# Low parts of mixer weights made by an accumulating transfer, a piece's low products last, and another plan for the order of work

## The chip, the core and the metric

The kernel runs on one core of a Trainium2 chip. The metric is the device time of one execution in microseconds (us), of which the median of several runs is taken. TensorE does the products, VectorE (DVE in the rows) and ScalarE (ACT) work on what lies in SBUF and PSUM, GpSimd (POOL) does small element-wise work and issues a few transfers, SyncE (SP) issues nearly all the others.

## The reference, cut to what matters

A trunk of two layers over 256 tokens of width 1024, all in float32. Of each layer the first statement, the mixer, is what this change is about.

```python
for i in range(DEPTH):                       # 2
    hn = rmsnorm(h, ln_mix[i])
    (g_q, g_k, g_v, g_z, g_a, g_b,
     n_q, n_kc, n_vc, n_ks, n_vs, n_kw, n_vw, n_gate,
     s_q, s_k, s_v) = jnp.split(hn @ w_in[i], SPLIT_POINTS, axis=-1)
    o_gdn = gated_deltanet(g_q, g_k, g_v, g_z, g_a, g_b, ...)   # 6 heads
    o_nsa = native_sparse_attention(n_q, ..., n_gate, ...)      # 6 query heads
    o_sb = stick_breaking_attention(s_q, s_k, s_v)              # 4 heads
    mix = jnp.concatenate([o_gdn, head_rmsnorm(o_nsa, ...), head_rmsnorm(o_sb, ...)], axis=-1)
    h = h + mix @ w_out[i]
    h = h + conv_ffn(rmsnorm(h, ln_ffn[i]), w_up[i], ffn_conv[i], w_down[i])
    gate = jax.nn.sigmoid(rmsnorm(h, ln_ple[i]) @ w_ple_gate[i])
    h = h + gate * rmsnorm(p[i] @ w_ple[i], ple_norm[i])
return rmsnorm(h, ln_final)
```

In `gated_deltanet` the tokens are cut into chunks of 64, and for each chunk and head a unit lower triangular system is solved before the chunks are run through one after the other.

## The kernel before, in words

**Products in three parts.** Float32 accuracy comes from three products of a cheaper type. Weights and activations are split into a high part (`wh_...`, `XH`) and a low part (`wl_...`, `XL`), and each product is high times high, high times low and low times high, added up in PSUM. A weight is read in pieces of 128 x 1024 (512 KB), in a fixed order: `g1` four times, `k` three times, `kcvc`, `g2`, `g3`, then `v v v q q q sq sq sk sk sv sv out ... ple ple` and the pieces of the feed-forward part.

**From memory to TensorE.** `prefetch` issues a piece's load on SyncE into one of five raw buffers (`wr_...`). `split_step` makes its two parts, in halves of 512 columns: ScalarE copies the raw piece into `wh_...`, which rounds it, and VectorE subtracts that from the raw piece into `wl_...`. There are four pairs of buffers for the parts. `take` hands a piece to the products, and sees to it that the next one (`LEAD` = 1) is split as well; `split_some` splits more as long as the clocks of ScalarE and VectorE in the program's own model are not more than `slack` ahead of TensorE's. `split_step` already has a second way to make a low part, for names in `ADDED`, and that tuple is empty: nothing goes that way in the kernel before.

**The order of the work.** Every engine works through its instructions in the order in which they are issued. The order is found when the program is built. Parts of the work are generators: the main one (priority 5) runs the projections, the out projection, the feed-forward part and the gate; others do the delta net (`gdn`, with `inverse` and `tokens` inside it), the sparse attention (`nsa`, `compress`, `cmp`, `heads`, `finish`) and the stick breaking (`sb`, `pair`). Each says what it waits for with `need`, and `drive` takes the ready one of the lowest priority number, by a model of the engines' clocks (`Model`). A projection says `need` once for each of its steps, so that its products fill the time in which the others wait. The numbers for each of the two layers stand in `PLAN`: priorities, `slack`, `fslack` (the slack of the feed-forward part), `early`, and `pace`, by which the projections go first when TensorE has had less to do.

**The substitution.** In `gdn`, `blocks` solves the diagonal 16 x 16 blocks of the triangular systems. It multiplies the products into `A`, writes `A` to memory (`D`), reads it back in another order (`Mb`), does 14 dependent pairs of small VectorE instructions (`prod`, `Tb`), and sends the result through memory once more (`Tq` to `G` to `F`), after which `stages` goes on. These transfers are issued on SyncE by `move`, in the same queue as the weights' loads.

**The order of the three products.** `pieceA` (weights stationary: `k`, `v`, `q`, `sq`, `sk`, and `ga` and `up` of the feed-forward part) and `piecesB` (activations stationary: `g2`, `g3`, `sv`) do the three products of one block of 128 rows after the other, and say `need` of the low part before each block.

Of the kernel before, what the change touches and what calls it, by code (L numbers as in the profile page):

```python
# [18 lines left out]
T = 256  # L19
D = 1024  # L20
KT = D // 128
HD = 64
# [116 lines left out]
def _prep(inp):  # L139

    f = lambda n: np.asarray(inp[n])
    out = {}
    out["x"] = f("x").reshape(T, D)
    out["pT"] = np.ascontiguousarray(
# [10 lines left out]
    for l in range(DEPTH):  # L155
# [10 lines left out]
                 "sq": col["sq"], "sk": col["sk"], "sv": col["sv"],  # L166
                 "out": np.concatenate([{0: wo[:384], 1: wo[768:], 2: wo[384:768].reshape(6, 64, D)[rg].reshape(384, D)}[i]
                                        for i in GROUPS[l]], axis=0),
# [26 lines left out]
class Model:  # L195
# [74 lines left out]
    def add(self, dst, src):  # L270

        t = max(self.clock["pool"], self.region(src)[0].max(), self.region(dst)[0].max()) + 0.8
        self.clock["pool"] = t
        self.landed(dst, src, t + self.ADD)

    ADD = 4.5

    def landed(self, dst, src, t):
        if "DRAM" not in str(src.space):
# [143 lines left out]
class Trunk:  # L423

    PLAN = (dict(pace=1.0, early=0.2, slack=5, fslack=6, step=1, gdn=0, nsa=0, sb=0, inverse=2,
                 tokens=3, out=0, compress=-1, cmp=2, heads=1, finish=1, pair=4),
            dict(pace=1.1, early=0.3, slack=3, fslack=8, step=1, gdn=1, nsa=0, sb=2, inverse=2,
                 tokens=3, out=2, compress=0, cmp=4, heads=3, finish=0, pair=2))  # L430
    WR = 5
    WARM = (14, 0, 1, 1, 1, 0)

    def __init__(self, ctx, tc, I, out, tap=None, depth=DEPTH):
# [32 lines left out]
        self.taken = []  # L467
        self.plan = self.M.plan = self.PLAN[0]
        self.slack = 0
# [178 lines left out]
    def spare(self, n, i):  # L648
        return (n, i) in self.SPARE

    ADDED = ()

    def added(self):
        return self.splitting[4] if self.splitting else self.n_split < len(self.split_seq) and self.by_transfer()

    def by_transfer(self):
        l, n, i = self.split_seq[self.n_split][:3]
        return n in self.ADDED and not self.spare(n, i) and self.n_split >= self.n_take + 2

    def split_to(self, n):  # L660
        while self.n_split < n:
# [6 lines left out]
               and self.split_step()):  # L668
            pass

    LEAD = 1

    def take(self, name, i):
        l = self.n_take // self.per_layer
        p = (l, name, i)
        while p not in self.parts:
            if not self.split_step():
                self.prefetch(now=True)
                assert self.split_step(), p
        self.n_take += 1  # L680
        self.taken.append(p)
        while self.n_split < min(self.n_take + self.LEAD, len(self.split_seq)) and not self.hold and self.split_step():
            pass
        return self.parts.pop(p)

# [7 lines left out]
    def setup(self):  # L693
        v, cp, I = self.v, self.cp, self.I
        self.table("silu_and_others")
        self.h = self.xp.tile([128, 2, D], F32, name="h")
        for s in self.HS:
# [69 lines left out]
    def row(self, i):  # L767

        while self.n_row <= min(i, 4 * self.depth):
            t = self.cp.tile([128, D], F32, tag="row", name=f"row{self.n_row}")  # L770
            j = self.n_row if self.n_row < 4 * self.depth else 4 * DEPTH
# [164 lines left out]
    def pieceA(self, name, i, out, X, fresh=False):  # L936

        W = self.take(name, i)
        if fresh:
            mm = self.t.matmul  # L940
            for k in range(KT):
                yield self.need(0, W[1], X[0])
                mm(out, W[0][:, k], X[0][:, k], start=k == 0, stop=False)
                mm(out, W[1][:, k], X[0][:, k], start=False, stop=False)
            for k in range(KT):
                mm(out, W[0][:, k], X[1][:, k], start=False, stop=k == KT - 1)
            self.done()
            return
        for k in range(0, KT, self.plan["step"]):
            yield self.need(0, W[1], X[1])  # L950
            self.projA(out, X, W, range(k, k + self.plan["step"]))
        self.done()

    def piecesB(self, name, n, outs, cols, X, nk):
        for i in range(n):
            W = self.take(name, i)
            for t in range(2):
                for k in range(nk):
                    yield self.need(0, W[1], self.of(t))
                    self.projB(outs[t][:, :cols], X, W, t, i * nk, [k])  # L960
            self.done()


# [226 lines left out]
    def gdn(self, l):  # L1190
        v, a, g, gp, c, m = self.v, self.a, self.g, self.gp, self.c, self.m
        mm = self.t.matmul
# [57 lines left out]
        for r, lhs, msk, dst in ((r1, "incl", "m_strict", dec), (r2, "gt", "m_incl", decT)):  # L1250
            for x in range(2):
# [3 lines left out]
                   start=False, stop=True)  # L1255
# [15 lines left out]
        def chunks(b, src, x):  # L1271

            for u, cp in units:
                t, hp = divmod(u, 3)
                o = t * 128 + cp * 64
                mm(b[P[cp], u * 64:u * 64 + 64], kn[P[x], hp, o:o + 64], src[P[x], hp, o:o + 64], start=True, stop=True)
# [3 lines left out]
        def blocks():  # L1280


            n = 24 * (64 // NB)
            M = gp.tile([n, NB, NB], F32, tag="h45_0", name="Mb")
            Tb = gp.tile([n, NB, NB], F32, tag="h45_1", name="Tb")
            g.memset(Tb, 0.0)
            g.memset(Tb.rearrange("p i c -> p (i c)")[:, ::NB + 1], 1.0)
            bs = yield self.small(2, kn, dec[0], dec[1])
            for x in range(2):
                chunks(bs[x], kn, x)  # L1290
            D = self.dram.tile([2, 6, 128, 64], F32, name=f"D{l}")
            for x in range(2):
                v.tensor_mul(fl(A[x]), bs[x][:, 0:384], fl(dec[x]))
            self.free(*bs)
            A16 = [H16("A16", "h1", x) for x in range(2)]
            for x in range(2):
                self.copy(A16[x], A[x])
            for x in range(2):
                yield self.need(0, A[x])
                self.move(D[x].rearrange("u p s -> p u s"), A[x])  # L1300
            yield self.need(0, D)
            nb = 64 // NB
            for k in range(nb):
                src = D.rearrange("x u (c b i) (e s) -> (x u c) b e i s", c=2, b=nb, e=nb)[:, k, k]
                self.move(M[k * 24:k * 24 + 24], src)
            prod = gp.tile([n, NB * NB // 4], F32, tag="h6_1", name="prod")
            yield self.need(0, M, Tb)
            for j in range(NB - 1):
                if j and j % 3 == 0:
                    yield self.pause(1)  # L1310
                r, c2 = NB - 1 - j, j + 1
                rows = M[:, j + 1:, j:j + 1]
                if j:
                    p = prod[:, 0:r * c2].rearrange("p (r c) -> p r c", c=c2)
                    v.tensor_tensor(p, rows.to_broadcast([n, r, c2]), Tb[:, j:j + 1, 0:c2].to_broadcast([n, r, c2]), op=OP.mult)
                else:
                    p = rows
                v.tensor_tensor(Tb[:, j + 1:, 0:c2], Tb[:, j + 1:, 0:c2], p, op=OP.subtract)
            G = self.dram.tile([2, 24, 64 // NB, NB, NB], F16, name=f"G{l}")
            F = gp.tile([128, 24, NB], F16, tag="h6_0", name="F")  # L1320
            Tqs = []
            for q in range(2):
                Tq = gp.tile([n, NB, NB], F16, tag=f"h0_{q}", name="Tq", bufs=2)
                v.tensor_copy(Tq, Tb if q == 0 else Tb.rearrange("p i c -> p c i"))
                Tqs.append(Tq)
            for q in range(2):
                yield self.need(0, Tqs[q])
                self.move(G[q].rearrange("r b i c -> b r (i c)"), Tqs[q].rearrange("p i c -> p (i c)"))
            yield self.need(0, G)
            for q in range(2):  # L1330
                self.move(F[:, q * 12:q * 12 + 12], G[q].rearrange("(z c) b i s -> (c b i) z s", c=2))
            yield self.need(0, F)
            return A16, F

        def stages(x, A16, F):
# [182 lines left out]
        for ch in range(4):  # L1518
            t, cp = divmod(ch, 2)
# [475 lines left out]
    def main(self):  # L1995
# [40 lines left out]
        for l in range(self.depth):  # L2036
            self.plan = self.M.plan = self.PLAN[l]
            self.slack = self.plan["slack"]
# [76 lines left out]
```

## Time and profile before

| | |
|---|---|
| median of 3 runs | 837.64 us (837.60 to 843.46) |
| the profiled execution | 837.27 us, of which the span from the first to the last instruction is 835.5 us |
| TensorE busy | 811.6 us, 97% of the span |
| VectorE busy | 626.3 us, 75% |
| ScalarE busy | 478.8 us, 57% |
| GpSimd busy | 77.4 us, 9% |
| mean granted clock of TensorE | 0.984 of full speed |

Busy time is the time in which an engine had an instruction of its own under way. A busy TensorE may still be at half its clock: the rows of stretches give the granted clock, where 1.00 is 2.4 GHz and 0.50 is 1.2 GHz.

### The profile page before, as it was taken

To read this page: it belongs to the slowest core of one execution; us is meant where nothing else is said; L and a number is where in the kernel's file an instruction comes from. 1 tells how busy PE (TensorE), PEld (TensorE's weight loads), DVE (VectorE), ACT (ScalarE), POOL (GpSimd) and SP (SyncE) were. 2 spreads that over 40 slices of the span, in tenths; PEclk is the share of its full clock that TensorE was granted. 3 is DMA by queue.
4 is the path that set the end of the run, shared out by engine and by line. 5 is a ranking of instruction groups with operands and counts; after the bars stand their busy time and mean duration, and the time that the engine had idled before them with its cause. 6 is when DMAs were issued, how large, how long until landed. Compare 5 with 4: busy or idle time off the path is not lost.

```text
span 835.5 us, 16816 instructions
## 1 busy us (share of the span) xinstructions
PE 811.6 (97%) x6529; PEld 736.3 (88%) x6529; DVE 626.3 (75%) x1337; ACT 478.8 (57%) x1043; POOL 77.4 (9%) x151
## 2 busy tenths in 40 slices
PE   8999899999999999999999979999999999999996
PEld 6989778888999999998998868888899999999986
DVE  5748988677887788876775688967588878788755
ACT  6546474556665566554655465627476556566543
POOL 2012000211100000000301100021110000000012
PEclk9999899999999999999999997999999999999999
DMA  8645230235676677753565414203446556676501
GB/s 310 251 163 150 66 110 28 77 123 154 201 227 186 188 214 220 218 189 96 152 233 186 134 69 111 86 27 102 151 152 227 202 181 202 220 209 219 176 30 51
DMA packets 50591, 131.40 MB, mean 157 GB/s; under 512 B 17104, under 2 KB 18000, under 8 KB 50512
## 3 DMA queue, kind: packets, MB, share of 16 engines
q1 hardware_dynamic: 49056, 125.42, 47.4%
q0 software_dynamic: 1312, 4.72, 1.7%
q8 instruction: 51, 0.84, 0.4%
q14 instruction: 28, 0.23, 0.1%
q10 hardware_dynamic: 144, 0.20, 0.1%
HBM read 128.29 MB, written 2.03 MB: 156 GB/s over the span
## 4 chain that ended last, share of the span: by engine, by line
PE 80%; DVE 10%; ACT 4%; DMA 2%; issue 2%; POOL 1%; SPq 0%; POOLq 0%; DVEq 0%; ACTq 0%
PE b L352 80%; DVE wl_g L352 1%; DMA wr_w1v<-in_w_dram 1%; DVE Tb L352 1%; DVE cv L352 1%; DVE prod L352 1%; DVE oq L352 1%; ACT XH L352 1%; DMA wr_g<-in_w_dram 1%; DVE XL L352 0%; DVE QQ L352 0%; DMA wr_q<-in_w_dram 0%; ACT xh L352 0%; ACT wh_g L352 0%; DVE wl_k L352 0%
## 5 line engine op out<-in xcount | busy, mean ns | idle before, releaser
L352 DVE SCALAR_TENSOR_TENSOR u<-b,pc,u 128x255 f32<-128x255 f32 (+1 forms) x176 | 84.7, 481 | 41.1 <-ACT u L352 37.9
L352 PE MATMUL b<-XL,wh_up 128*128 128x256 f32 x352 | 99.7, 283 | 0.0
L352 PE MATMUL b<-XH,wl_up 128*128 128x256 f32 x352 | 99.6, 283 | 0.0
L352 PE MATMUL b<-XH,wh_up 128*128 128x256 f32 x352 | 99.6, 283 | 0.0
L352 PE MATMUL b<-XH,wl_ga 128*128 128x256 f32 x352 | 99.0, 283 | 0.0
L352 PE MATMUL b<-XH,wh_ga 128*128 128x256 f32 x352 | 99.0, 283 | 0.0
L352 PE MATMUL b<-XL,wh_ga 128*128 128x256 f32 x352 | 97.3, 283 | 0.0
L352 ACT ACTIVATE u<-b,pc 128x256 f32<-128x256 f32 x88 | 41.5, 472 | 74.8 <-PE b L352 74.8
L352 PE MATMUL b<-wl_dn,ah 128*128 128x512 f32 x176 | 69.3, 394 | 0.0
L352 PE MATMUL b<-wh_dn,al 128*128 128x512 f32 x176 | 69.2, 393 | 0.0
L352 PE MATMUL b<-wh_dn,ah 128*128 128x512 f32 x176 | 69.2, 393 | 0.0
L352 PEld LDWEIGHTS b<-XH,wh_ga 128*128 128x128 f32 x352 | 66.9, 190 | 1.7
L352 PEld LDWEIGHTS b<-XL,wh_ga 128*128 128x128 f32 x352 | 66.0, 190 | 1.5
L352 PEld LDWEIGHTS b<-XL,wh_up 128*128 128x128 f32 x352 | 67.1, 191 | 0.0
L352 PEld LDWEIGHTS b<-XH,wh_up 128*128 128x128 f32 x352 | 67.1, 191 | 0.0
L352 PEld LDWEIGHTS b<-XH,wl_up 128*128 128x128 f32 x352 | 67.1, 191 | 0.0
L352 PEld LDWEIGHTS b<-XH,wl_ga 128*128 128x128 f32 x352 | 67.0, 190 | 0.1
L352 DVE TENSOR_TENSOR wl_ga<-wr_ga,wh_ga 128x512 fp32r<-128x512 f32 x88 | 56.9, 688 | 6.1 <-ACT wh_ga L352 2.6
L352 DVE TENSOR_TENSOR wl_up<-wr_up,wh_up 128x512 fp32r<-128x512 f32 x88 | 56.6, 685 | 0.4
L352 DVE TENSOR_TENSOR wl_dn<-wr_dn,wh_dn 128x512 fp32r<-128x512 f32 x88 | 56.5, 684 | 0.4
L352 ACT ACTIVATE ah<-sg 128x256 fp32r<-128x256 f32 x44 | 18.4, 418 | 64.8 <-DVE sg L352 64.8
L352 ACT ACTIVATE wh_up<-wr_up 128x512 fp32r<-128x512 f32 x88 | 50.2, 620 | 0.0
(385 smaller groups left out, 2209.7 us busy)
## 6 DMA issues: line engine op xcount, KB each, us to landing
wr_ga<-in_w_dram SPq DMA_DIRECT2D x44, 512.0 KB, 3.8
wr_up<-in_w_dram SPq DMA_DIRECT2D x44, 512.0 KB, 4.2
wr_dn<-in_w_dram SPq DMA_DIRECT2D x44, 512.0 KB, 3.6
wr_out<-in_w_dram SPq DMA_DIRECT2D x16, 512.0 KB, 3.5
wr_pg<-in_w_dram SPq DMA_DIRECT2D x16, 512.0 KB, 3.3
row<-in_rows_dram POOLq DMA_DIRECT2D x8, 512.0 KB, 4.1
wr_g<-in_w_dram SPq DMA_DIRECT2D x8, 512.0 KB, 5.5
wr_g<-in_w_dram SPq DMA_DIRECT2D x8, 414.0 KB, 3.3
```

Of the source, the lines that this page charges most:

```text
L352: return f(*args, **kw)
```

## The change

- `ADDED` names `v`, `q`, `sq`, `sk` and `sv`. For a piece that goes this way ScalarE writes the high part and then its negative into the low part's buffer, and GpSimd issues one transfer of the whole piece that adds the raw piece to it. VectorE does nothing.
- A piece goes this way only if it is at least two pieces behind the next one to be taken, if the model's clock of the loads and of GpSimd is less than `ROOM` = 0.5 us ahead of ScalarE's, and if `quiet` is off. `quiet` is set from the write of `A` until `Mb` is there, and from the tenth step of the substitution until `F` is there.
- With such a piece next, `take` looks three pieces ahead instead of one.
- `Model.add` puts a transfer into the clock of the loads.
- `pieceA` and `piecesB` do all products with the high part of a weight first and those with its low part last, and say `need` of each part on its own, a block at a time.
- `PLAN` has other numbers for both layers.

```diff
@@ Model.add
         t = max(self.clock["pool"], self.region(src)[0].max(), self.region(dst)[0].max()) + 0.8
         self.clock["pool"] = t
-        self.landed(dst, src, t + self.ADD)
-
-    ADD = 4.5
+        self.loaded = t = max(self.loaded, t + 1.2) + 2.7
+        self.landed(dst, src, t + 0.9)
@@ Trunk
-    PLAN = (dict(pace=1.0, early=0.2, slack=5, fslack=6, step=1, gdn=0, nsa=0, sb=0, inverse=2,
+    PLAN = (dict(pace=1.0, early=0.2, slack=2, fslack=6, step=1, gdn=3, nsa=4, sb=0, inverse=0,
                  tokens=3, out=0, compress=-1, cmp=2, heads=1, finish=1, pair=4),
-            dict(pace=1.1, early=0.3, slack=3, fslack=8, step=1, gdn=1, nsa=0, sb=2, inverse=2,
-                 tokens=3, out=2, compress=0, cmp=4, heads=3, finish=0, pair=2))
+            dict(pace=1.2, early=0.05, slack=2, fslack=8, step=1, gdn=1, nsa=1, sb=-2, inverse=2,
+                 tokens=3, out=2, compress=4, cmp=4, heads=3, finish=0, pair=4))
...
-    ADDED = ()
+    ADDED = ("v", "q", "sq", "sk", "sv")
+
+    ROOM = 0.5
+    quiet = False
...
     def by_transfer(self):
         l, n, i = self.split_seq[self.n_split][:3]
-        return n in self.ADDED and not self.spare(n, i) and self.n_split >= self.n_take + 2
+        return n in self.ADDED and not self.spare(n, i) and not self.quiet and self.n_split >= self.n_take + 2 \
+            and max(self.M.loaded, self.M.clock["pool"]) < self.M.clock["act"] + self.ROOM
...
-    LEAD = 1
+    LEAD = 3
@@ take
-        while self.n_split < min(self.n_take + self.LEAD, len(self.split_seq)) and not self.hold and self.split_step():
+        while self.n_split < min(self.n_take + (self.LEAD if self.added() else 1), len(self.split_seq)) and not self.hold and self.split_step():
             pass
@@ pieceA
-        for k in range(0, KT, self.plan["step"]):
-            yield self.need(0, W[1], X[1])
-            self.projA(out, X, W, range(k, k + self.plan["step"]))
+        mm = self.t.matmul
+        for k in range(KT):
+            yield self.need(0, W[0], X[1])
+            for x in X:
+                mm(out, W[0][:, k], x[:, k], start=k == 0 and x is X[0], stop=False)
+        for k in range(KT):
+            yield self.need(0, W[1])
+            mm(out, W[1][:, k], X[0][:, k], start=False, stop=k == KT - 1)
         self.done()
@@ piecesB
+        mm = self.t.matmul
         for i in range(n):
             W = self.take(name, i)
-            for t in range(2):
-                for k in range(nk):
-                    yield self.need(0, W[1], self.of(t))
-                    self.projB(outs[t][:, :cols], X, W, t, i * nk, [k])
+            for q, xs in ((0, X), (1, X[:1])):
+                for t in range(2):
+                    s = slice(t * 128, t * 128 + 128)
+                    for k in range(nk):
+                        yield self.need(0, W[q], self.of(t))
+                        self.M.part = t
+                        for x in xs:
+                            mm(outs[t][:, :cols], x[:, i * nk + k, s], W[q][:, k], start=(q, i, k) == (0, 0, 0) and x is X[0],
+                               stop=(q, i, k) == (1, n - 1, nk - 1))
+                        self.M.part = None
             self.done()
@@ gdn, blocks
             D = self.dram.tile([2, 6, 128, 64], F32, name=f"D{l}")
+            self.quiet = True
...
             yield self.need(0, M, Tb)
+            self.quiet = False
             for j in range(NB - 1):
+                self.quiet = j >= 9
...
             yield self.need(0, F)
+            self.quiet = False
             return A16, F
```

## Rows read from the trace of the kernel before

**Rows 1.** The page: the span and the busy time of each engine.
```profile
span 835.5 us, 16816 instructions
PE 811.6 (97%) x6529; PEld 736.3 (88%) x6529; DVE 626.3 (75%) x1337; ACT 478.8 (57%) x1043; POOL 77.4 (9%) x151
```
**Rows 2.** Stretches: from:to, length, busy time (instructions) by engine, clock, DMA share, GB/s.
```profile
20.00:81.00 61.00, 60.66 (x450) 55.61 (x449) 39.84 (x100) 34.40 (x74) 7.59 (x14) 1.00 0.60 199
81.00:113.00 32.00, 28.05 (x185) 23.45 (x186) 30.23 (x92) 16.85 (x41) 1.37 (x3) 0.89 0.32 89
113.00:170.00 57.00, 56.21 (x868) 48.80 (x867) 42.19 (x109) 32.29 (x64) 8.02 (x14) 1.00 0.19 58
...
485.00:512.00 27.00, 21.93 (x127) 18.76 (x127) 25.45 (x77) 11.18 (x27) 0.92 (x2) 0.75 0.26 67
...
612.00:800.00 188.00, 188.00 (x1324) 176.63 (x1325) 150.80 (x282) 113.62 (x241) 3.81 (x8) 1.00 0.61 197
```
**Rows 3.** Stretches of the first layer's mixer, the same columns.
```profile
94.00:98.00 4.00, 1.95 (x14) 1.43 (x12) 3.69 (x14) 2.55 (x5) 0.00 (x0) 1.00 0.07 20
98.00:105.00 7.00, 6.27 (x27) 5.33 (x28) 6.76 (x18) 2.78 (x7) 0.91 (x2) 0.51 0.63 129
105.00:108.00 3.00, 2.10 (x13) 1.27 (x12) 2.83 (x8) 0.87 (x3) 0.40 (x1) 1.00 0.73 231
```
**Rows 4.** Stretches of the second layer's mixer, the same columns.
```profile
485.00:494.00 9.00, 8.56 (x69) 7.84 (x68) 8.25 (x25) 3.71 (x7) 0.00 (x0) 1.00 0.01 4
...
494.00:499.00 5.00, 0.39 (x3) 0.19 (x3) 4.55 (x20) 2.35 (x7) 0.00 (x0) 0.84 0.01 2
499.00:511.00 12.00, 11.98 (x50) 9.73 (x51) 11.65 (x33) 5.12 (x15) 0.50 (x2) 0.50 0.58 147
```
**Rows 5.** Waits of TensorE, the whole run: in total, times, longest (us).
```profile
PE b L352 <- DVE mx L352: 4.6, 1, 4.6
PE b L352 <- DVE cq L352: 1.7, 1, 1.7
```
**Rows 6.** VectorE's groups, 81 to 113 us, then 485 to 512: busy us, mean ns.
```profile
L352 DVE TENSOR_TENSOR wl_q<-wr_q,wh_q 128x512 fp32r<-128x512 f32 x4 | 2.6, 682 | 0.0
L352 DVE TENSOR_TENSOR wl_sk<-wr_sk,wh_sk 128x512 fp32r<-128x512 f32 x4 | 2.6, 685 | 0.0
L352 DVE TENSOR_TENSOR wl_sq<-wr_sq,wh_sq 128x512 fp32r<-128x512 f32 x4 | 2.6, 681 | 0.0
...
L352 DVE TENSOR_TENSOR wl_q<-wr_q,wh_q 128x512 fp32r<-128x512 f32 x4 | 2.6, 683 | 0.0
L352 DVE TENSOR_TENSOR wl_sq<-wr_sq,wh_sq 128x512 fp32r<-128x512 f32 x3 | 1.9, 687 | 0.0
```
**Rows 7.** ScalarE's copies: a group of 485 to 512 us; the chain near 480 us.
```profile
L352 ACT ACTIVATE wh_q<-wr_q 128x512 fp32r<-128x512 f32 x4 | 2.3, 620 | 0.0
...
480.49 1.14 ACT wh_q L352 x2
```
**Rows 8.** The substitution by its tiles: duration min/median/max ns, first and last start us.
```profile
L352 DVE TENSOR_TENSOR prod<-Mb,Tb x28: 172/206/222, 85.3 to 496.8; 96x28 f32<-96x28 f32 x4, 96x39 f32<-96x39 f32 x4, 96x48 f32<-96x48 f32 x4, 96x55 f32<-96x55 f32 x4
L497 SPq DMA_DIRECT2D Mb<-D x8: 322/415/430, 66.9 to 472.9; - x8
```
**Rows 9.** GpSimd's loads of 512 KB by their tile: issue in ns, landing in us.
```profile
L772 POOL DMA_DIRECT2D row<-in_rows_dram x8: 613/635/788, 17.3 to 808.0; - x8
DMA to landing us min/median/max: 3.9/4.1/7.4
```
**Rows 10.** TensorE in order of time, 84 to 89 us: start, duration, operation.
```profile
84.68 0.28 PE L352 MATMUL b<-XH,wh_q 128*128 128x256 f32 x1
...
87.80 0.28 PE L352 MATMUL b<-XH,wl_q 128*128 128x256 f32 x1
...
88.27 0.36 PE L352 MATMUL b<-XH,wh_q 128*128 128x256 f32 x1
88.47 0.28 PE L352 MATMUL b<-XL,wh_q 128*128 128x256 f32 x1
```

## The prediction

> **What bounds the kernel now.** I read the page first. TensorE is busy for 811.6 of 835.5 us, and no other engine for more than 75% [rows 1], so time can only be won where TensorE stands or runs at its lower clock. The stretches come next. In the feed-forward part it works without a gap at full clock, 188.00 of 188.00 us in the second layer [rows 2]; one of two such rows stands, for the first layer's is alike. In the mixers two stretches stand out. From 81 to 113 us it is busy for 28.05 of 32 us at a mean clock of 0.89, from 485 to 512 us for 21.93 of 27 us at 0.75, and in both VectorE is nearly full: 30.23 of 32 and 25.45 of 27 us [rows 2]. What follows is full again, 56.21 of 57 us at clock 1.00 [rows 2]; so is the stretch behind the second one (again one of two rows).
>
> A finer cut prices them. First layer: TensorE stands for 2.05 us in 94 to 98, 0.73 in 98 to 105 and 0.90 in 105 to 108, and 6.27 busy us run at 0.51 [rows 3]. That is 2.4 GHz in part and 1.2 in the rest, mostly the latter: 6.27 x 0.49 = 3.1 us lost to the clock, 3.7 to waiting, together 6.8. Second layer: 4.6 us of standing in 494 to 499, then 11.98 busy us at 0.50, so 6.0 lost to the clock, together 10.6 [rows 4]. The clock fell each time after TensorE had stood. The sum, 17.4 us, is all that the change can win in these stretches: 837.27 - 17.4 = 819.9. The waits say for what TensorE stood: 4.6 us for VectorE's `mx`, 1.7 for its `cq` [rows 5]. Both are instructions that came late in a full queue, behind the substitution among others.
>
> **The change, part by part.**
>
> *Subtractions leave VectorE.* In 81 to 113 us it makes 12 half low parts of `q`, `sq` and `sk`, 12 x 0.68 = 8.2 us (7.8 within the stretch), in 485 to 512 us seven, 4.5 us [rows 6]. At best all go. At worst none does: a piece has to be two behind the next one taken, with four pairs of buffers and one piece in use, so only one or two can be eligible at a time, and `quiet` shuts the way from `A` to `Mb` and again from the tenth step to `F`. What is left open during the substitution are its first nine steps, about 9 x 2 x 0.24 = 4 us of VectorE's queue (206 ns each and a gap, [rows 8]).
>
> *What TensorE could do meanwhile.* From 485 to 494 us ScalarE is busy for 3.71 of 9 us, the transfers for 1% [rows 4]. A piece's 24 products of 256 columns are 0.12 us apart (27 of them from 84.68 to 87.80 us, [rows 10]), so 2.9 us. Two pieces of `q` made there would be 5.8 us of work, more than the 4.6 us of standing, and all of the 10.6 us would come back. With one piece, 2.9 us are filled; the rest, 1.7 us, is like the first layer's 2.05, after which still 3.1 us went to the clock [rows 3]: 2.9 + (6.0 - 3.1) = 5.8 us. Ends 0 and 10.6; I take 8, between one and two pieces. In the first layer one piece covers the 2.05 us, but the nine subtractions behind it lie mostly where `quiet` forbids transfers until `F`. Ends 0 and 6.8; I take half, 3.4. Sum: 11.4 us won.
>
> *What is added on ScalarE.* Two more copies a piece, nearest row 0.62 us each [rows 7]. In the full stretches ScalarE has room (16.85 of 32 and 11.18 of 27 us, [rows 2]), which hides them. Without cover they cost 1.24 us a piece: near 480 us the copies of `wh_q`, 1.14 us, stand on the chain ahead of the attention's operands [rows 7]. Ends 0 and 2.4 a layer; I take 0.6, so 1.2.
>
> *The transfers.* Issue on GpSimd takes 0.61 to 0.79 us; a plain load of 512 KB from there lands after 3.9 to 7.4 us, mostly 4.1 [rows 9]. No row shows one that adds. It moves at least as much as a load and reads a second operand, so its ends are 3.9 and twice the slowest, 14.8; sooner than a load is excluded. I take 5, nearest to the median load. There is time for that: two pieces ahead, 5.8 us, and 16 products of the piece itself, 1.9 us, make 7.7; less copies and issue (1.24 and 0.64) 5.8 us are left. So nothing is lost, but only by 0.8 us. GpSimd waits at the transfer for ScalarE's copies, and behind it in the queue wait the additions of the rope, the products of the delta state and the norms' powers, with VectorE waiting for those; GpSimd is busy for 9% [rows 1], and I take nothing, at worst 1.2 us a piece. The raw buffer stays held some 5 us longer. The next load waits for it on SyncE, and the substitution's own transfers are queued behind that load. From 485 to 494 us that queue carries nothing [rows 4].
>
> The Trainium skill (SBUF — State Buffer, Who interferes with whom) speaks against transfers from GpSimd: their descriptors are written through a port that VectorE can hold for a whole instruction in its two-port modes. The eight issues in [rows 9] took 0.61 to 0.79 us, so the trace does not bear out a long wait. By the rule an issue would wait for at most one such instruction, some tenths of a microsecond by estimate, which would bring the 0.8 us down and makes the late transfer below a little likelier.
>
> *Low products last.* The three kinds take equally long and each has its own weight load, so the order alone costs nothing in the full stretches, the feed-forward part among them (1324 products in 188 us, [rows 2]). It lets TensorE begin 1.9 us before a low part is there. Steps become shorter: two products or one instead of three. After another kind of work the first product takes 0.20 us instead of 0.12 [rows 10], so every added return to the projections costs 0.08. Ends: none, or 30 returns, 2.4 us; I take 0.6.
>
> *The plan.* The first layer's substitution comes forward. Its data is asked for at 66.9 us (issue of `Mb`), but its first `prod` starts at 85.3 [rows 8], because the attention's operands were put ahead. With `inverse` at 0 and `nsa` at 4 it can start up to 14 us sooner, while VectorE has room: from 20 to 81 us it is busy for 39.84 of 61, and TensorE for 60.66 [rows 2]. That supports the half which I took. It delays the sparse attention by the substitution's 10 us, which the projections can cover. `slack` 2 instead of 5 and 3 leaves VectorE's queue shorter, and also fewer pieces ready ahead. I can't price an order that I don't see: at best it brings the rest of the 17.4 us, at worst a new stall of the size of the second layer's, 10.6 us. I take nothing.
>
> Sum: 837.27 - 11.4 + 1.2 + 0.6 = 827.7 us. The profiled execution lies 0.37 us below the median of 837.64, so **828 us**.
>
> **The rivals.**
>
> *The relief changes nothing* (time 835, 832 to 841). Pieces are not eligible when it counts, or the stall only moves: with the projections used up earlier, `mx`, the convolutions and the substitution still follow each other on VectorE, and a later stretch starves. For it: in 485 to 498 us VectorE did no subtraction at all, so removing subtractions can't shorten that queue; and the second layer's `inverse` stays at 2. Against it: TensorE stood although ScalarE and the transfers were idle, just what the second way uses. It would give the 3.4 us of one layer or less, 834 to 838.
>
> *The transfer comes late* (time 848). If it lands more than 5.8 us after its issue, TensorE stands at the low products, in order, with everything behind it. At 7.4 us, the slowest row, that is 1.6 us for each piece; with 9.5 pieces in the two stretches (19 half parts, [rows 6]) 15 us. Since 2 us of standing was enough to bring the clock down [rows 3], some 5 us more go to the clock. 828 + 15 + 5 = 848. It decides from 5.8 us of landing on, and is worth more than the gain from about 6.8. For it: two operands and a queue shared with weight loads. Against it: the transfers were 1% busy from 485 to 494 us.
>
> *It does not do what it says*: no transfer at all. Then the order and the plan act alone, within the first rival's span; it is counted there.
>
> **How the numbers follow.** A measurement of this kernel can tell about 1%, 8.4 us, from no change, so faster means below 829.2 and slower above 846. Forecast (820 to 833 us): 0.55, of which 0.40 below 829.2, since its middle lies there and the ends of the second layer are nearer to the full 10.6 than to none. The relief that changes nothing: 0.25, all within 1%. Late transfers: 0.20, above 846. Together faster 0.40, same 0.40, slower 0.20. The range takes in the ceiling (819.9, and 0.9 for the unknown plan) and the second rival; late transfers stay outside: 819 to 846.
>
> **What would show it.** Right: `wl_q`, `wl_sq`, `wl_sk` or `wl_sv` written by GpSimd's transfers, five to ten a layer; fewer VectorE subtractions near the substitution; no waits of several us for `mx` or `cq`; no stretch of 12 us at 0.50 in the second layer; the first `prod` well before 85 us. Wrong: TensorE waiting for a `wl` from a transfer (late); the same number of subtractions (not done); TensorE standing after 150 or after 550 us, where it is full now (the stall moved); ScalarE's copies ending the chain ahead of the attention. A landing time of 8 us or more, or fewer than three transfers a layer, would make the forecast wrong.

## The result and the profile after

The changed kernel takes 834.48 us (median of 20 runs, 831.96 to 839.93), the kernel before 837.85 us beside it (20 runs). The ratio is 0.9941, with a 95% interval of 0.9915 to 0.9966: a gain of 0.6%, within the 1% that was called no change. Executions of one program differ with their mean granted clock: of 35 of the kernel before, measured beside no_transfers, 16 took 836.1 to 838.0 us at 0.983 to 0.987 and 12 took 842.9 to 844.4 us at 0.977 or 0.978. The profiled execution took 832.23 us. The forecast of 828 was too low, and the time is that of the first rival (835).

The page of the kernel after, first its span and engines, which answer to [rows 1]:

```profile
span 830.4 us, 16809 instructions
PE 805.0 (97%) x6529; PEld 730.2 (88%) x6529; DVE 622.2 (75%) x1332; ACT 482.6 (58%) x1048; POOL 80.3 (10%) x156
```

VectorE is busy for 4 us less than its 626, ScalarE for as much more. Then the stretches of the kernel after, with the columns of [rows 2]:

```profile
81.00:113.00 32.00, 28.97 (x310) 24.56 (x311) 30.17 (x91) 18.88 (x46) 2.27 (x5) 1.00 0.25 60
485.00:512.00 27.00, 26.37 (x234) 22.80 (x234) 24.61 (x58) 21.18 (x47) 1.47 (x3) 1.00 0.41 116
575.00:590.00 15.00, 9.24 (x29) 6.09 (x28) 7.41 (x17) 3.67 (x9) 2.72 (x4) 0.67 0.32 107
612.00:800.00 188.00, 187.75 (x1322) 176.08 (x1321) 148.49 (x278) 111.45 (x239) 3.63 (x9) 1.00 0.60 193
```

Both stretches that cost 17.4 us before are nearly mended: the clock is 1.00 in each, TensorE stands for 3.03 us in the first and 0.63 in the second. That is 3.7 us left, 13.7 won; in the first stretch most of what is won is the clock's 3.1 us, since 3.03 us of standing are left of 3.95. The third row is new. From 575 to 590 us TensorE stands for 5.76 us, and 9.24 busy us run at 0.67 (3.0 us lost), together 8.8. In the kernel before this stretch was full:

```profile
575.00:590.00 15.00, 15.00 (x94) 12.78 (x93) 11.16 (x24) 10.24 (x25) 3.11 (x5) 1.00 0.33 108
```

13.7 won and 8.8 given back leave 4.9, and the span is 5.1 us shorter. The feed-forward row is as full as before. TensorE's longest wait of the kernel after is no longer for `mx` [rows 5] but for the last output of the delta net, followed by short ones:

```profile
PE b L351 <- DVE zs L351: 3.3, 1, 3.3
PE b L351 <- ACT XH L351: 1.8, 5, 0.7
PE b L351 <- ACT wh_q L351: 1.6, 1, 1.6
```

**Why 575 to 590 starves.** The substitution of the kernel after answers to [rows 8], and two later tiles of the delta net's chain stand beside it, the state `S` and the gated output `zs`:

```profile
L351 DVE TENSOR_TENSOR prod<-Mb,Tb x28: 171/206/242, 76.2 to 481.8; 96x28 f32<-96x28 f32 x4, 96x39 f32<-96x39 f32 x4, 96x48 f32<-96x48 f32 x4, 96x55 f32<-96x55 f32 x4
L351 DVE TENSOR_TENSOR S<-S,b x4: 347/355/356, 148.1 to 566.1; 128x192 f32<-128x192 f32 x4
L351 DVE TENSOR_TENSOR zs<-oq,zs x8: 357/358/358, 154.2 to 584.6; 128x192 f32<-128x192 f32 x8
```

The same two tiles of the kernel before:

```profile
L352 DVE TENSOR_TENSOR S<-S,b x4: 348/353/354, 159.7 to 557.2; 128x192 f32<-128x192 f32 x4
L352 DVE TENSOR_TENSOR zs<-oq,zs x8: 357/358/358, 168.8 to 583.2; 128x192 f32<-128x192 f32 x8
```

In the first layer everything comes sooner. In the second the last `prod` starts 15.0 us sooner (481.8 for 496.8), but the last `S` starts 8.9 us later and the last `zs` 1.4 later. TensorE used the head start up on projections: the last product with `wl_sv` starts at 555.2 us, where before it started at 577.1. When the projections were done it had to wait for `zs`, as late as ever, which the out projection takes before stick breaking's rows. VectorE's order of time in the kernel after shows where the delta net stuck (a gap in brackets is idle time and what ended it):

```profile
549.67 0.63 DVE L351 TENSOR_TENSOR vn<-uu,b 64x192 f32<-64x192 f32 x2
553.50 0.55 DVE L351 TENSOR_REDUCE hss<-hsq 128x6 f32<-128x384 f32 x1 [3.20 <-ACT hsq L351]
555.80 0.86 DVE L351 TENSOR_TENSOR o<-o,hss 128x384 f32<-128x384 f32 x1 [1.74 <-POOL hss L351]
556.67 1.95 DVE L351 SCALAR_TENSOR_TENSOR L<-b,L 128x384 f32<-128x384 f32 x4
558.54 0.75 DVE L351 TENSOR_TENSOR pl<-pT,ph 128x256 fp32r<-128x256 f32 x2
559.20 2.49 DVE L351 TENSOR_TENSOR wl_out<-wr_out,wh_out 128x512 fp32r<-128x512 f32 x4
561.61 0.35 DVE L351 TENSOR_TENSOR S<-S,b 128x192 f32<-128x192 f32 x1
```

Between `vn` and the `S` that follows it in the chain lie 11.9 us. Two more lines show that VectorE's queue is only half of it. This `S` also needs a product of `vn` on TensorE and a step on GpSimd:

```profile
555.44 0.56 PE L351 MATMUL b<-vn,kk 64*64 64x64 f32 x12
```

```profile
555.74 0.50 POOL L351 TENSOR_TENSOR S<-S,eg 128x192 f32<-128x192 f32 x1
```

The product comes behind 5 us of `sv`'s products in TensorE's order, GpSimd's step behind the sparse attention's norm. So `S` could not go before 556.2 us, and the 4.94 us for which VectorE idles before that norm's two steps are not what held it. From then on it stood for 5.4 us more in VectorE's queue, behind stick breaking (`L`), the low part `pl` and a piece of `out`. Behind the late `zs`, 575 to 590 us gives back 8.8 of the 13.7 us won; TensorE waits for no transfer there.

**What became of the transfers.** The DMA issues of the kernel after, then the issue on GpSimd and ScalarE's negating copies of one tile:

```profile
wl_sk<-wr_sk POOLq DMA_DIRECT2D x2, 512.0 KB, 5.7
wl_sv<-wr_sv POOLq DMA_DIRECT2D x2, 512.0 KB, 4.9
wl_q<-wr_q POOLq DMA_DIRECT2D x1, 512.0 KB, 4.7
```

```profile
L351 ACT ACTIVATE wl_sk<-wh_sk x4: 630/632/633, 110.0 to 119.6; 128x512 fp32r<-128x512 f32 x4
L630 POOL DMA_DIRECT2D wl_sk<-wr_sk x2: 865/898/931, 112.1 to 120.6; - x2
```

Only five of 24 pieces went that way, three in the first layer and two in the second. In the two stretches VectorE still makes 18 half low parts (8 and 10) where it made 19 [rows 6], and it is as full as before: 30.17 of 32 us, and 24.61 of 27. It was not relieved.

### The profile page after: what moved, and what is told of

It reads as the page before. It is cut to its first block, busy times and chain, and to the rows that moved or that the text cites. A ratio compares the mean times of both kernels' runs of the same rounds, so it can differ in the third digit from the quotient of the medians.

```text
span 830.4 us, 16809 instructions
## 1 busy us (share of the span) xinstructions
PE 805.0 (97%) x6529; PEld 730.2 (88%) x6529; DVE 622.2 (75%) x1332; ACT 482.6 (58%) x1048; POOL 80.3 (10%) x156
## 4 chain that ended last, share of the span: by engine, by line
PE 80%; DVE 9%; ACT 6%; POOL 2%; issue 2%; POOLq 0%; DVEq 0%; ACTq 0%
PE b L351 80%; POOL hss L351 1%; ACT XH L351 1%; DVE oq L351 1%; DVE wl_out L351 1%; DVE XL L351 1%; DVE wl_v L351 1%; POOL ss L351 1%; ACT wh_q L351 0%; ACT L472 0%; ACT KH L351 0%; ACT xh L351 0%; DVE wl_k L351 0%; ACT ctmp L351 0%; DVE ck L351 0%
## 5 line engine op out<-in xcount | busy, mean ns | idle before, releaser
L351 PE MATMUL b<-XH,wh_up 128*128 128x256 f32 x352 | 86.4, 283 | 0.0
L351 PE MATMUL b<-XL,wh_up 128*128 128x256 f32 x352 | 86.4, 283 | 0.0
L351 PE MATMUL b<-XH,wh_ga 128*128 128x256 f32 x352 | 86.2, 282 | 0.0
L351 PE MATMUL b<-XL,wh_ga 128*128 128x256 f32 x352 | 84.6, 283 | 0.0
L351 PE MATMUL b<-XH,wl_ga 128*128 128x256 f32 x352 | 51.1, 283 | 0.0
L351 ACT ACTIVATE wh_dn<-wr_dn 128x512 fp32r<-128x512 f32 x88 | 50.2, 621 | 0.0
L351 ACT ACTIVATE wh_ga<-wr_ga 128x512 fp32r<-128x512 f32 x88 | 50.1, 617 | 0.0
L351 PE MATMUL b<-XH,wl_up 128*128 128x256 f32 x352 | 49.4, 283 | 0.0
```

Source lines behind the costliest of these rows:

```text
L351: return f(*args, **kw)
```

## The experiments

All ratios are to the kernel before, with 95% intervals. What a stretch loses is TensorE's standing plus its busy time times what the clock lacks, as above.

### Which part makes the gain

**no_transfers**: the kernel after without transfers.

```diff
-    ADDED = ("v", "q", "sq", "sk", "sv")
+    ADDED = ()
```

> The changed kernel with ADDED empty: plan and low products last stay, the five transfers become VectorE subtractions. If the plan made the gain (theory of the order: the changed trace has only five transfers, ten half subtractions of 0.68 us), within 2 us of the changed kernel, ratio to before 0.992 to 0.997. If the transfers made it (theory of the relief, the forecast's), it falls back to before, ratio 0.999 to 1.003, and the stand of 4.6 us for mx with about 12 us at clock 0.50 is there again.

834.51 us (12 runs), 0.9944 [0.9913, 0.9974]: the same as after. The transfers are worth nothing that can be measured, in either direction. But the loss lies elsewhere: 575 to 590 is nearly full here, and a late stall with its stand for `zs` (3.8 us) is in the first layer:

```profile
170.00:190.00 20.00, 15.33 (x80) 11.49 (x80) 11.51 (x27) 7.18 (x15) 4.61 (x6) 0.85 0.30 98
575.00:590.00 15.00, 14.82 (x110) 12.39 (x104) 11.88 (x28) 8.33 (x19) 4.28 (x6) 1.00 0.39 125
```

**plan_only**: the kernel before with the new `PLAN` and nothing else.

```diff
-    PLAN = (dict(pace=1.0, early=0.2, slack=5, ..., gdn=0, nsa=0, inverse=2, ...), dict(...))
+    PLAN = (dict(pace=1.0, early=0.2, slack=2, ..., gdn=3, nsa=4, inverse=0, ...), dict(...))
```

> The kernel before with the new PLAN alone: products in the old order, no transfers, the model without transfers. Theory of the order: most of the gain, ratio 0.992 to 0.998. Theory of the relief: no gain or a loss, ratio 0.999 to 1.010, because the slack of 2 leaves fewer pieces ready and nothing takes work from VectorE.

834.85 us (12 runs), 0.9942 [0.9913, 0.9972]: by the ratio the plan alone gives as much as the whole change. Its profiled execution, 836.88 us, is only 0.4 us below the 837.27 of the kernel before, so the profiles do not bear out a gain of this size. Nor are the stretches the same:

```profile
81.00:113.00 32.00, 28.46 (x211) 24.08 (x210) 26.30 (x76) 14.85 (x38) 1.38 (x3) 0.79 0.28 73
485.00:512.00 27.00, 23.17 (x195) 21.50 (x194) 24.56 (x74) 16.01 (x35) 0.92 (x2) 1.00 0.37 110
```

The second layer's 10.6 us are down to 3.8, the first layer's 6.8 have become 9.5 (3.5 standing, 28.46 x 0.21 of clock); the waits are for VectorE's `wl_q` (5.5 us, three times), which the order of the products then removes.

**low_last_only**: the kernel before with only the new `pieceA` and `piecesB`.

```diff
-            yield self.need(0, W[1], X[1])
-            self.projA(out, X, W, range(k, k + self.plan["step"]))
+            yield self.need(0, W[0], X[1])
+            ... (high products; then the low ones, each behind need(0, W[1]))
```

> The kernel before with the new pieceA and piecesB alone. Theory of the order: the plan is needed, ratio 0.998 to 1.002. Third theory (low products last is what counts, since TensorE can begin a piece 1.9 us before its low part is there): ratio 0.993 to 0.997, and the stand before mx gets shorter by 2 us or more in the second layer.

847.3 us (12 runs), 1.0087 [1.0054, 1.0121]: slower. In the profiled execution the span is 10.6 us longer (846.1), and 8.5 us are lost where the kernel before loses nothing: from 455 to 480 us TensorE is busy for 24.93 us at 0.66, a fall of the clock without a stand (see the end). The order alone also brings new waits, for VectorE's `cv` (3.7 us), `zs` (2.9) and `oq` (1.9), which the kernel before did not have at this length, while 485 to 512 us loses 4.2 us for 10.6. What the shorter steps cost by themselves, for which 0.6 us was taken, is not separated from the clock.

**old_product_order**: the kernel after with the old `pieceA` and `piecesB` (the diff above, turned round).

> The changed kernel with the pieceA and piecesB of before, so a low part is wanted with the first block of its piece; seven pieces go by transfer (sq, sk, sv and q, sk, sv, sv). If low products last is needed to cover the transfers' 5 to 6 us, TensorE stands for a wl from a transfer and the ratio to before is 0.997 to 1.005. Theory of the order: two pieces ahead are cover enough, ratio 0.990 to 0.996, the same as the plan alone (0.994).

837.4 us (12 runs), 0.9974 [0.9940, 1.0007]. With plan and transfers the low products last may be worth 0.3%, but the intervals overlap (0.9940 to 0.9966 lies in both), and without the transfers, plan and old order had 0.9942, so this is not shown. Seven pieces go by transfer here. It waits for `wl_q` again (4.3 us of VectorE's, 0.9 of a transfer's).

**all_but_plan**: the kernel after with the old `PLAN`.

> The changed kernel with the PLAN of before: four transfers (q and sv in each layer), low products last. Theory of the order: no gain, ratio 0.997 to 1.004. Theory of the relief: most of the gain, 0.992 to 0.997, and the stand of the second layer mostly gone.

835.27 us (12 runs), 0.9965 [0.9932, 0.9997]. That is 1.2% below low_last_only's 1.0087, with four transfers and their longer look ahead as the only difference. In 81 to 113 us TensorE is now busy for 29.88 of 32 us at a clock of 1.00 (2.1 us lost), with low last alone for 28.85 at 0.84 (7.8 lost). But low_last_only's profiled execution had lost 8.5 us to its clock from 455 to 480 us, where this one is at 1.00, so how much of the 1.2% the transfers win stays open. By the ratios the parts do not add up: the order costs 0.9% alone and nothing that shows with the rest. And here too a late stall comes, with the old plan: from 170 to 190 us TensorE is busy for 15.04 of 20 us at 0.76, 8.6 us lost, its longest wait `zs` (2.1 us).

### Which layer's plan, and the late stall

**plan_first_layer** (the kernel after, second layer's numbers of before) and **plan_second_layer** (the other way round).

```diff
@@ plan_first_layer
-            dict(pace=1.2, early=0.05, slack=2, fslack=8, step=1, gdn=1, nsa=1, sb=-2, ..., compress=4, ..., pair=4))
+            dict(pace=1.1, early=0.3, slack=3, fslack=8, step=1, gdn=1, nsa=0, sb=2, ..., compress=0, ..., pair=2))
```

> The changed kernel with the new PLAN for the first layer alone; the second layer has the numbers of before. Theory of the order: the first layer's 4 us stay, and the second layer stands neither as before nor at its end: ratio to before 0.988 to 0.996, its late stand for zs at most 2 us. Theory that any plan of the second layer loses the same (the loss only moves): 0.994 to 1.000, with 8 to 12 us of standing and half clock somewhere in the second mixer.

> The changed kernel with the new PLAN for the second layer alone. Theory of the order: the first layer loses its gain again, 6 to 7 us of standing and half clock in 90 to 110 us or later; the second layer ends about as in the changed kernel, with its late stand for zs: ratio 0.995 to 1.002.

The first layer's plan alone took 830.11 us (4 runs), 0.9892 [0.9834, 0.9950], the second layer's alone 832.69 us (10 runs), 0.9920 [0.9892, 0.9948]: neither half needs the other, and the second's result missed its expectation. With the old numbers in the second layer the last `zs` starts at 575.5 us and the late stall is gone, while 485 to 512 us loses 5.2 us again (23.19 of 27 us busy at 0.94):

```profile
575.00:590.00 15.00, 14.95 (x69) 11.98 (x68) 8.91 (x19) 7.44 (x15) 2.41 (x4) 1.00 0.41 132
```

With the old numbers in the first layer the stall goes to 170 to 190 us instead (15.53 of 20 us busy at 0.74). There 575 to 590 us is nearly full (14.41 of 15 us at 1.00), although the second layer has the numbers of the kernel after. So the late stall is not a property of one layer's numbers.

**stick_before_delta**: the kernel after, the out projection of the second layer taking stick breaking's rows before the delta net's.

```diff
-GROUPS = ((2, 0, 1), (2, 0, 1))
+GROUPS = ((2, 0, 1), (2, 1, 0))
```

> The changed kernel; in the second layer the out projection takes the stick breaking's rows before the delta net's (24 products of 512 columns, 0.23 us each, 5.5 us that don't wait for zs). If the gain was given back at the late stand for zs (3.3 us, and 3 us at clock 0.50 behind it), the stand vanishes and the time falls by 5 to 7 us from the changed kernel: ratio to before 0.985 to 0.989. If TensorE's end is set by the delta net's chain however the products lie, the same time as the changed kernel, 0.992 to 0.997.

832.70 us (4 runs, 827.23 to 832.96), 0.9895 [0.9822, 0.9967]. The wait for `zs` is gone, one for stick breaking's `XL` (2.0 us) is there, and 575 to 590 loses 3.3 us (1.97 standing, 13.03 x 0.10) for 8.8:

```profile
575.00:590.00 15.00, 13.03 (x73) 9.72 (x72) 10.16 (x24) 6.69 (x14) 3.62 (x5) 0.90 0.32 105
```

So the order in the out projection did make TensorE wait there. The profiled execution (832.96 us) shows no gain all the same, for a reason of the clock that is told at the end, and the interval takes in both expectations: that the time falls is not shown.

**stick_first_slack_5**: the same, with `slack` 5 in the first layer against its short waits for `wh_g` and `wh_q`.

> The changed kernel with the stick breaking's rows before the delta net's in the second layer's out projection, and slack 5 instead of 2 in the first layer's plan; four transfers. If the slack of 2 is what lets TensorE stand 1.5 us for wh_g near 36 us and 1.6 us for wh_q near 85 us, both vanish and the time falls by 2 to 3 us below the swapped order alone (827.2 in its undisturbed run): 824 to 826 us, ratio 0.983 to 0.987. If the stands only move, 827 to 832 us, ratio 0.987 to 0.994.

835.46 us (12 runs), 0.9949 [0.9922, 0.9976]; the 824 to 826 were missed. Those short waits went, and a stand of 4.3 us for `zs` came in the first layer: 170 to 190 us is busy for 14.98 of 20 us at 0.83. The second layer, whose numbers did not change, loses 5.9 us from 575 to 590 (11.81 us busy at 0.77) where the swapped order had lost 3.3. One number of the plan reorders everything behind it.

### What the transfers do, and what holds them back

**all_by_transfer**: all 24 pieces by transfer.

```diff
-    ROOM = 0.5
+    ROOM = 50.0
...
-        return n in self.ADDED and not self.spare(n, i) and not self.quiet and self.n_split >= self.n_take + 2 \
+        return n in self.ADDED and not self.spare(n, i) and self.n_split >= self.n_take + 2 \
```

> The changed kernel without the two conditions on room and on the substitution: all 24 pieces by transfer, 48 half subtractions of 0.68 us or 33 us fewer on VectorE. Theory of the relief: each us taken from VectorE in its full stretches counts, ratio 0.980 to 0.992. Theory of the late transfer (a rival of the forecast): landing rises from 4.7 to 5.7 us to over 8, the substitution's own transfers wait as well, TensorE stands for wl parts: ratio 1.00 to 1.03. Theory of the order: the low parts were not what TensorE stood for, so ratio 0.992 to 1.005.

849.91 us (4 runs), 1.0107 [1.0039, 1.0176]: the rival of the late transfer, at its 848. Its DMA issues, a stretch, and two waits of TensorE:

```profile
wl_q<-wr_q POOLq DMA_DIRECT2D x6, 512.0 KB, 8.4
wl_sq<-wr_sq POOLq DMA_DIRECT2D x4, 512.0 KB, 8.7
F<-G SPq DMA_DIRECT2D x4, 48.0 KB, 9.4
```

```profile
495.00:520.00 25.00, 17.29 (x142) 16.06 (x141) 12.99 (x30) 19.24 (x40) 4.23 (x5) 0.94 1.07 246
```

```profile
PE b L351 <- DVE Ab L351: 13.4, 2, 8.4
PE b L351 <- DMA wl_q<-wr_q: 3.1, 3, 2.4
```

Here VectorE's queue is short at last (12.99 of 25 us busy, 21.61 in the same stretch of the kernel before), and it doesn't help, because VectorE stands for `F` for 9.1 of the other 12 us. The DMA share is 1.07, and the substitution's own transfers are under way among the big ones: `F` lands after 9.4 us where the kernel before has 4.2. TensorE stands 13.4 us for `Ab`, which is not made from `F` but comes behind `Ta` and `TTa` in VectorE's queue, and these are; it stands 5.4 us for the low parts themselves (3.1 for `wl_q`, 2.3 for `wl_v`). The harm is real, but most of it is not where the rival had put it.

**no_quiet** and **no_room**: the kernel after with one of the two conditions taken away (the second and the first part of that diff).

> The changed kernel with transfers allowed during the substitution too, the condition on room kept: six transfers (q, sq, sk, sv; q, sv). If it is the company of transfers that delays the substitution's own ones (with all by transfer F landed after 7.4 to 13 us instead of 2.7 to 4.5), F lands late in the first layer, 6 us or more, and the ratio is 0.996 to 1.004. If only their number does it, F lands as before and the ratio is 0.991 to 0.996.

> The changed kernel without the condition on room, the one on the substitution kept: seven transfers (sk, sk, sv, sv; q, sv, sv). Two more transfers, away from the substitution: landing 5 to 7 us, nobody waits for them, ratio 0.990 to 0.997 by the theory of the order; if room counts, landing over 8 us and TensorE stands for a wl, 0.998 to 1.005.

Without `quiet`: 836.42 us (12 runs), 0.9942 [0.9912, 0.9972], six transfers, `F` lands after 2.9 us. With so few transfers `quiet` protects from nothing that shows. Without `ROOM`: **825.99 us** (6 runs, 823.35 to 830.15), 0.9834 [0.9787, 0.9880], better than both kernels and beyond its expectation. It has seven transfers, the two more being the other pieces of `sv`. The four of `sv`, the stretch that starved, and the tile that came late:

```profile
wl_sv<-wr_sv POOLq DMA_DIRECT2D x4, 512.0 KB, 5.3
```

```profile
575.00:590.00 15.00, 15.00 (x69) 12.37 (x68) 8.15 (x16) 6.13 (x11) 1.20 (x2) 1.00 0.64 182
```

```profile
L351 DVE TENSOR_TENSOR zs<-oq,zs x8: 357/358/359, 154.4 to 570.4; 128x192 f32<-128x192 f32 x8
```

The last `zs` starts at 570.4 us for 584.6, and the stretch that cost 8.8 us costs nothing; the span is 8.9 us shorter (821.5). The two further transfers save VectorE two half subtractions in each layer, 1.4 us, which can't make 14 us by itself. But with another split the builder's clocks differ, and so the order on all engines. VectorE's order of time now has `S` 1.4 us behind its `vn`, not 11.9:

```profile
548.61 0.63 DVE L351 TENSOR_TENSOR vn<-uu,b 64x192 f32<-64x192 f32 x2
549.96 0.35 DVE L351 TENSOR_TENSOR S<-S,b 128x192 f32<-128x192 f32 x1 [0.72 <-PE b L351]
```

Which of the two did it these runs don't separate.

## Why the prediction was right or wrong

- **The two stretches and their price: right.** Their 17.4 us were what could be won there, and 13.7 were. That this lies near the 11.4 that I took is luck: the 11.4 were worked out from transfers that hardly ran. In the second layer the stand of 4.6 us is gone and the half clock with it. In the first TensorE still stands for 3.03 us, the longest wait 1.6, and the clock stays at 1.00; so "2 us of standing was enough to bring the clock down", from the late transfer's price, holds for the kernel before and not here.
- **"Subtractions leave VectorE": wrong cause.** 18 half parts stayed where 19 had been, since only three and two pieces met the conditions; fewer than three a layer was named as what would make the forecast wrong. no_transfers shows it: no transfer at all, and in its first stretch the clock is 1.00 too. What goes with the mended stretches is the plan with the low products last: the substitution began 9 us sooner in the first layer (`prod` at 76.2 for 85.3) and ended 15 sooner in the second (481.8 for 496.8). In the first layer neither does it alone: the plan alone leaves 9.5 us lost there and low last alone 7.8, low last with the plan 3.0 (no_transfers), with the transfers 2.1 (all_but_plan, where they do help). In the second layer the plan alone leaves 3.8 of the 10.6, low last alone 4.2 (22.78 of 27 us at 1.00).
- **"I take nothing" for a new stall: the term that failed.** The sum had it under the plan, with 10.6 us as its worst end, and it came: 8.8 us at 575 to 590. 837.27 - 13.7 + 8.8 = 832.4, and the profiled execution took 832.23. It does not belong to the plan alone either: all_but_plan, with the old numbers, loses 8.6 us at 170 to 190. What the sum left out is that when the projections run ahead they are used up sooner, while the second layer's last `zs` comes no sooner (584.6 for 583.2). The first rival had this mechanism ("a later stretch starves") and the time; it went wrong only in that the first stall would stay. The range held, but it is wide enough (819 to 846) for the forecast and this rival alike.
- **ScalarE's copies: right in size** (0.63 us each for 0.62), and only GpSimd waited for them: it stood for 11.1 us before `wl_sk`'s two transfers and 12.7 before `wl_sv`'s. That is more than the 1.2 a piece that I had as worst, but no wait of TensorE ends on GpSimd.
- **Landing: right.** I took 5 us; it was 4.7 to 6.6, and no TensorE wait ends on it. The Trainium skill (DMA: Bandwidth & Descriptors, Anatomy of one DMA — SWDGE (gpsimd) path) gives 2.0 us and the bytes at 436 GB/s, 3.2 us for 512 KB by estimate. The runs do not bear that out for a transfer that adds. An issue took 0.87 to 0.93 us for the 0.61 to 0.79 of the plain loads [rows 9].
- **The late transfer: not in this kernel, true without its conditions.** It needs both to be gone, and most of the price lies in `F` (13.4 us of standing behind it, 5.4 for the low parts).
- **Low products last at 0.6 us: open.** Alone they were 0.9% slower, 8.5 us of it in the profile a fall of the clock that may not be theirs; with the rest no price shows. The feed-forward part was right: 187.75 of 188 us.

## What to carry to other kernels

Before crediting a mechanism, count how many items its conditions let through; here five of 24, and leaving them out left the time where it was (0.9944 for 0.9941). A reordering that mends one stall hands the time to the next chain that has not moved, so follow the saved work to the last consumer: when the projections run ahead but the delta net's end does not, much of the gain is lost there. When the order is found by a model, parts are not additive, and single numbers of a plan should be judged by lost TensorE time per stretch, not by one total.

## What was not expected of the hardware

- TensorE's clock fell without it having stood. stick_before_delta's instructions for TensorE are those of the kernel after up to the second layer's out projection, yet in one stretch they ran differently, without a gap in either (first the kernel after):

```profile
45.00:62.00 17.00, 17.00 (x155) 14.39 (x155) 8.84 (x18) 7.70 (x17) 0.49 (x3) 1.00 0.46 149
```

```profile
45.00:62.00 17.00, 17.00 (x93) 14.11 (x92) 6.69 (x13) 4.64 (x11) 0.87 (x3) 0.70 0.40 133
```

  17.00 x 0.30 is 5.1 us, about what the mended stall had won. There TensorE does small products (32 of 45 columns for each of two weights, 287 and 289 ns each in the kernel after; in stick_before_delta those of the second weight take 377). In low_last_only the same happened from 455 to 480 us (24.93 of 25 us busy at 0.66), during the same 64 small products of the second layer, and in no_quiet from 45 to 62 us (17.00 of 17.00 us busy at 0.60). What sets it off is open; a profile of one execution can hide or feign 5 to 8 us in this way.
- Transfers of 512 KB that add land after 7.5 to 8.7 us in the median where many follow each other (`v`, `q` and `sq` of all_by_transfer) instead of 4.7 to 5.7, and bring small ones of 48 KB from 4.2 to 9.4.
